# The last load group of a DMA-bound batched product: 112 rows and four pieces of 4 rows in place of 128 rows

## The chip, the cores and the metric

One core of one Trainium2 chip. The metric is the device time of one execution in microseconds (us); lower is better. The span of a profile is some 1.8 us shorter than the device time of the same run. Words used below: SBUF is the on-chip memory of 128 partitions, HBM the memory outside, SP the engine (SyncE) whose queue issues the DMAs; a row is what one DMA engine moves in one packet, to or from one partition; a landing is the event by which one DMA engine reports its share of a DMA as done, in us from the start of the span.

## The reference

```python
x: (8, 12, 512, 64) float32      y: (8, 12, 512, 64) float32
out = np.einsum('bhtc,bhsc->bhts', x, y)      # (8, 12, 512, 512) float32
```

25.2 MB are read and 100.7 MB written: 96 products of 512x64 by 64x512, each of which writes four times what it reads.

## The kernel before

The 96 heads are cut into 12 groups of 8. A group's x is 128 rows of 8 KB, one row per partition, and y likewise; both go into one slot of 16 KB per partition, of which there are five. Slots hold loads first and results afterwards. All DMAs are issued by SP.

```python
P = 128; G = 8; R = 32; NG = 12; SLOTS = 5        # C = 64, S = 512, K = 8
slots = ctx.enter_context(tc.tile_pool(name="slots", bufs=SLOTS))
...
def load(g):
    both = slot()
    nc.sync.dma_start(both[:, :R * C], xv[g])      # 128 rows of 8 KB
    nc.sync.dma_start(both[:, R * C:], yv[g])      # 128 rows of 8 KB
    loaded[g] = both
...
    # result(o): 8 matmuls, three copies from PSUM into a slot, and then
    return lambda: nc.sync.dma_start(ov[i, h], otf)    # 128 rows of 16 KB
...
for g in range(SLOTS):
    load(g)
...
for g in range(NG):                # compress each group to bf16 and load on
    ...
    if g < 5: load(g + SLOTS)
    elif g in (5, 7, 9): stores.append(result(len(stores)))
    elif g in (6, 8): load(g // 2 + 7)      # g == 8: the last group, 11
for store in stores:               # three finished results wait for the loads
    store()
for o in range(len(stores), 4 * NG):
    result(o)()
```

So all loads come first and all 48 stores after them, and group 11 is the last load on the queue.

## Time and profile before

| | before |
|---|---|
| time, 6 runs | 302.11 us (301.77 to 302.23) |
| profiled span | 300.3 us |
| bytes | 125.83 MB on one queue |
| a load row of 8 KB | 309 to 321 ns in one DMA engine |
| a store row of 16 KB | 611 ns in one DMA engine |

The prediction shows the lines that say that the DMA engines are the bound. One view is added here: the stretch in which the last loads run, cut into microseconds. Columns: stretch and length, busy time and count of PE, PEld, DVE, ACT and POOL, TensorE clock, mean busy share of the 16 DMA engines, GB/s. Kernel before:

```profile
57.00:58.00 1.00, 0.00 (x0) 0.00 (x0) 1.00 (x2) 0.92 (x2) 0.95 (x1) 0.50 0.99 410
58.00:59.00 1.00, 0.00 (x0) 0.00 (x0) 1.00 (x2) 1.00 (x2) 0.98 (x1) 0.50 1.08 451
59.00:60.00 1.00, 0.85 (x3) 0.30 (x3) 0.99 (x2) 1.00 (x2) 0.94 (x2) 0.50 0.97 401
60.00:61.00 1.00, 1.00 (x4) 0.34 (x3) 1.00 (x1) 1.00 (x2) 1.00 (x1) 0.50 1.06 442
61.00:62.00 1.00, 1.00 (x4) 0.33 (x3) 0.71 (x1) 0.98 (x2) 0.96 (x2) 0.50 1.00 401
62.00:63.00 1.00, 0.49 (x2) 0.10 (x1) 0.00 (x0) 1.00 (x1) 0.90 (x1) 0.97 1.22 508
63.00:64.00 1.00, 0.00 (x0) 0.00 (x0) 0.82 (x2) 0.98 (x2) 0.80 (x1) 1.00 0.92 393
64.00:65.00 1.00, 0.00 (x0) 0.00 (x0) 1.00 (x1) 0.97 (x2) 1.00 (x1) 1.00 0.92 393
```

A busy share above 1 only means that packets are counted in the slice in which they start.

### The profile page before, as it was taken

What the parts mean: (1) busy time and instruction counts of PE and PEld (TensorE: products, weight loads), DVE (VectorE), ACT (ScalarE), POOL (GpSimd) and SP (SyncE); (2) the same over time, 40 slices, a digit from 0 to 9 for tenths busy, and PEclk for the clock granted to TensorE, in tenths of its full rate; (3) what the DMA queues carried; (4) which work ended last, traced back from release to release, by engine and by line L of the source; (5) the groups of instructions that cost most, each with busy time, mean ns of one, the idle gap of its engine ahead of it and who ended that gap; (6) DMA issues with size and microseconds to landing.
All of it is one profiled execution on the core that took longest, in us unless ns stands there. A gap on an engine that the chain in (4) does not pass through costs nothing.

```text
span 300.3 us, 1412 instructions
## 1 busy us (share of the span) xinstructions
PE 145.4 (48%) x377; PEld 46.5 (15%) x384; DVE 182.6 (61%) x160; ACT 221.3 (74%) x169; POOL 59.1 (20%) x56
## 2 busy tenths in 40 slices
PE   0004044138657484856475656655674655673000
PEld 0001011012212121212121212211121211120000
DVE  1568895989984963947909649289195570603200
ACT  4666599998999779789789697888887977364000
POOL 2899999990000000000000000000000000000000
PEclk9999995676978659567957566779657788577555
DMA  7999999999999999999999999999999999999994
GB/s 281 430 421 421 422 423 420 426 429 440 421 431 436 419 436 434 421 436 432 420 450 423 423 439 423 432 439 421 436 432 423 426 438 423 420 421 441 426 430 205
DMA packets 10377, 125.93 MB, mean 419 GB/s; under 512 B 1152, under 2 KB 1152, under 8 KB 1152
## 3 DMA queue, kind: packets, MB, share of 16 engines
q1 hardware_dynamic: 10368, 125.83, 98.8%
q8 instruction: 3, 0.05, 0.1%
q14 instruction: 6, 0.05, 0.0%
HBM read 25.17 MB, written 100.66 MB: 419 GB/s over the span
## 4 chain that ended last, share of the span: by engine, by line
DMA 53%; ACT 11%; DVE 7%; issue 1%; DVEq 1%; PE 0%; ACTq 0%
DMA out_dram<-slot 53%; ACT slot L66 8%; DVE slot L68 7%; ACT xb L66 2%; ACT xk L83 1%; DVEq L192 1%; PE pm L135 0%; ACT yb L66 0%; DVE yb L68 0%; DVEq L68 0%; ACTq L66 0%
## 5 line engine op out<-in xcount | busy, mean ns | idle before, releaser
L135 PE MATMUL pm<-yT,xT 128*128 128x512 bf16 x377 | 145.4, 524 | 129.7 <-ACT slot L66 74.3
L66 ACT ACTIVATE slot<-pm 128x1536 f32<-128x1536 f32 (+1 forms) x108 | 133.2, 1314 | 37.9 <-DMA out_dram<-slot 27.7
L68 DVE COPY slot<-pm 128x1536 f32<-128x1536 f32 (+1 forms) x36 | 54.6, 1571 | 72.5 <-DMA out_dram<-slot 38.0
L135 PEld LDWEIGHTS <-xT 128*128 128x128 bf16 x384 | 46.5, 121 | 227.7 <-issue 194.0
L116 DVE STREAM_TRANSPOSE xT<-xb 128x1024 uint32<-128x1024 uint32 x24 | 48.8, 2034 | 6.2 <-PE pm L135 4.6
L66 ACT ACTIVATE xb<-xk 32x1024 bf16<-32x1024 bf16 x36 | 48.2, 1338 | 0.8
L68 DVE CAST yb<-slot 64x1024 bf16<-64x1024 f32 x24 | 33.8, 1408 | 17.6 <-DMA slot<-in_y_dram 17.3
L68 POOL COPY xb<-xk 32x1024 bf16<-32x1024 bf16 x24 | 38.5, 1606 | 1.2
L83 ACT ACTIVATE xk<-slot 128x2048 bf16<-128x2048 f32 x12 | 22.9, 1910 | 9.6 <-DMA slot<-in_x_dram 9.5
L68 DVE COPY xb<-xk 32x1024 bf16<-32x1024 bf16 x36 | 26.1, 725 | 0.4
L121 DVE STREAM_TRANSPOSE yT<-yb 128x512 uint32<-128x512 uint32 x24 | 25.1, 1044 | 0.0
L68 POOL CAST yb<-slot 64x1024 bf16<-64x1024 f32 x12 | 19.2, 1601 | 7.4 <-DMA slot<-in_y_dram 6.8
L66 ACT ACTIVATE yb<-slot 64x1024 bf16<-64x1024 f32 x12 | 15.9, 1329 | 3.6 <-DMA slot<-in_y_dram 3.5
L83 ACT ACT_TABLE_LOAD x1 | 1.3, 1283 | 0.7 <-PEq L181 0.7
L149 DVE MEMSET xb<- 128x64 uint32 x16 | 1.2, 112 | 0.8 <-PEq L181 0.8
L150 POOL MEMSET xb<- 128x64 uint32 x16 | 1.4, 151 | 0.3 <-POOLq L181 0.3
L181 POOL MEMSET const-float32-0.0<- 128x1 f32 x1 | 0.1, 98 | 0.2 <-issue 0.2
L181 POOL MEMSET const-float32-1.0<- 128x1 f32 x1 | 0.1, 98 | 0.0
L181 POOL MEMSET const-bfloat16-1.0<- 128x1 bf16 x1 | 0.1, 98 | 0.0
L181 POOL MEMSET const-uint8-127<- 128x1 uint8 x1 | 0.1, 98 | 0.0
## 6 DMA issues: line engine op xcount, KB each, us to landing
out_dram<-slot SPq DMA_DIRECT2D x48, 2048.0 KB, 20.6
slot<-in_x_dram SPq DMA_DIRECT2D x12, 1024.0 KB, 17.5
slot<-in_y_dram SPq DMA_DIRECT2D x12, 1024.0 KB, 19.3
```

Source lines behind the costliest of these rows:

```text
L66: nc.scalar.activation(dst, src, COPY)
L68: engine.tensor_copy(dst, src)
L83: nc.scalar.activation(xk.rearrange("p r c -> p (r c)"), both[:, :R * C], COPY)
L116: nc.vector.transpose(xT.rearrange("p (k r e) -> p k e r", k=K, e=E), xb.rearrange("p (k e c) -> p k e c", k=K, e=E),)
L121: nc.vector.transpose(yT.rearrange("p (r j) -> p j r", r=D), yb.rearrange("p (j c) -> p j c", c=D))
L135: nc.tensor.matmul(pm[:, j, :], xT[:, k + j, h, :], yT[:, h * S:(h + 1) * S], start=True, stop=True)
L149: nc.vector.memset(zeroed[0][:, k:k + 64], 0.0)
L150: nc.gpsimd.memset(zeroed[1][:, k:k + 64], 0.0)
L181: nc = _bacc.Bacc("TRN2", target_bir_lowering=False, num_devices=1)
L192: with _tile.TileContext(nc) as tc:
```

## The change

The intent follows from the sizes: the 16 DMA engines do not finish together, so 16 of the 128 rows of the last x and of the last y are taken off the even split and sent in pieces of 4 rows, each carried by four engines (that they are engines 0 to 3 is what the page says that the prediction cites, the records carry no numbers).

```diff
     def load(g):
         both = slot()
-        nc.sync.dma_start(both[:, :R * C], xv[g])
-        nc.sync.dma_start(both[:, R * C:], yv[g])
+        for src, dst in ((xv[g], both[:, :R * C]), (yv[g], both[:, R * C:])):
+            cuts = (0, P) if g < NG - 1 else (0, P - 16, P - 12, P - 8, P - 4, P)
+            for lo, hi in zip(cuts[:-1], cuts[1:]):
+                nc.sync.dma_start(dst[lo:hi], src[lo:hi])
         loaded[g] = both
```

## The prediction

> **What bounds the kernel now.** I read the page first: is one engine full, or the DMA?
>
> ```profile
> PE 145.4 (48%) x377; PEld 46.5 (15%) x384; DVE 182.6 (61%) x160; ACT 221.3 (74%) x169; POOL 59.1 (20%) x56
> ...
> DMA  7999999999999999999999999999999999999994
> ...
> q1 hardware_dynamic: 10368, 125.83, 98.8%
> ...
> DMA 53%; ACT 11%; DVE 7%; issue 1%; DVEq 1%; PE 0%; ACTq 0%
> ```
>
> No compute engine is over 74%, and the DMA row is full from the second slice to the next to last: the one queue's packets fill 98.8% of 16 engines' span. The chain names compute at places (ACT 11%), but only because compute waits for a slot which a store frees. So the span is start-up, 16 DMA engines' time for 125.83 MB, and a tail. The question for a change of 16 rows is how that work lies over the 16 engines, so I cut the end into pieces of 1 us (columns: stretch, then busy time and count of PE, PEld, DVE, ACT, POOL, clock, DMA share, GB/s):
>
> ```profile
> 290.00:296.00 6.00, 0.00 (x0) 0.00 (x0) 0.00 (x0) 0.00 (x0) 0.00 (x0) 0.50 1.02 434
> 296.00:297.00 1.00, 0.00 (x0) 0.00 (x0) 0.00 (x0) 0.00 (x0) 0.00 (x0) 0.50 0.23 98
> 297.00:298.00 1.00, 0.00 (x0) 0.00 (x0) 0.00 (x0) 0.00 (x0) 0.00 (x0) 0.50 0.15 66
> 298.00:299.00 1.00, 0.00 (x0) 0.00 (x0) 0.00 (x0) 0.00 (x0) 0.00 (x0) 0.50 0.04 16
> ```
>
> The engines do not end together: after 296 us some 4, then 2 to 3, then one of 16 still move data. The raw landing events say it more finely. Each DMA has 16 landings, one per engine. For the loads the first and last of them lie 0.32 to 0.36 us apart; for the last store ten engines land within 0.27 us, four at 0.90 to 1.06 us, one at 2.28 and one at 3.02 us. That one engine sets the end. The packet records say where its lag comes from: a store row (16 KB) takes 611 ns and a load row (8 KB) 309 ns, but three 16 KB instruction packets took 968, 967 and 948 ns, and single engines fall back by about as much when these pass. Engine numbers are not in the records.
>
> The last place to read is where the changed loads go, on the SP queue:
>
> ```profile
> 54.33 0.33 SPq L75 DMA_DIRECT2D slot<-in_x_dram  x1
> 54.71 0.42 SPq L76 DMA_DIRECT2D slot<-in_y_dram  x1
> 55.19 15.47 SPq L143 DMA_DIRECT2D out_dram<-slot  x4
> ```
>
> At 54.33 us the group before is still in the engines: landings complete at 55.37 (x of group 10), 57.84 (its y), 60.33 (x of group 11), 63.15 (its y), 68.02 us (store 0). No hole: 2.5 us per load (8 rows of 309 ns) and 4.87 per store (8 of 611).
>
> **What the Trainium skill says.** "DMA: Bandwidth & Descriptors", section "Why a DMA increments its semaphore by 16 and not by 1": a DMA is spread over the largest k up to 16 which divides its outer dimension, on the lowest-numbered k engines. 128 rows give 8 to each of 16, 112 give 7, and 4 rows go to engines 0 to 3, one each. The trace agrees for 128 rows (16 landings per DMA, 8 rows each); it has no 4-row DMA. The same page, "Latency and other measured facts", calls engines 7 and 15 usually slower, for a reason given as a guess. Two engines do lag most here, but nothing tells their numbers. "Runtime: NRT & Kernel Launch", section "Instruction fetch mechanics", has instruction memory refilled in 16 KiB blocks by the sequencer's own DMA queue; the three 16 KB packets are such blocks. "SBUF — State Buffer", section "Door 1: The DMA port swizzle", puts four neighbouring partitions on one DMA port, measured at 27.6 GB/s for partitions 0 to 3; no DMA of this trace is that narrow.
>
> **The change part by part.** The same bytes, otherwise dealt. Removed: two DMAs of 128 rows. Added: two of 112 and eight of 4, so 80 DMAs and not 72.
>
> 1. Rows. Per load, engines 4 to 15 get 7 and not 8; engines 0 to 3 get 7 + 4 = 11. For x and y together that is 2 rows less on twelve engines, 2 x 309 = 0.62 us, and 6 more on four engines, 6 x 309 = 1.85 us. The queue is never dry afterwards (a store takes 20.6 us from issue to landing, over four stores of 4.87), so these shifts should last to the end as lags do. If engines 0 to 3 are among the ten punctual ones, they end at up to 0.27 + 1.85 = 2.1 us on the old scale, the last laggard at 3.02 - 0.62 = 2.4: the end comes 0.6 us sooner. That is plainly the intent, and the size fits the measured lags well.
>
> 2. Issue. Eight more instructions on the SP queue, some 0.4 us each (0.33 to 0.42 above): 3.2 us, before the first store. The built order adds waits: eight semaphores are used in turn, so each DMA waits for the eighth before it. The third y piece waits for the 112 rows of x, the fourth for x's first piece, store 0 for x's second. From 57.84 us, x's 112 rows take 7 x 309 = 2.16 us, landing at about 60.0; the pieces follow 0.31 us apart, so the third y piece goes out at 60.1, the fourth at 60.5, store 0 at about 61.0. The first DMA of the run had its first packet 1.0 us after its issue began, so store 0 moves data from 62.0. Engines 4 to 15 have ended y's 112 rows at 60.0 + 2.16 = 62.2 on the landing clock, some 0.4 us earlier as packets (the last packet ends 0.46 us before the last landing). So they may stand dry 0.2 to 0.5 us, which eats half or more of the 0.6.
>
> 3. Later arrival. y of group 11 lands on engines 0 to 3 about 1.85 us later, near 65.0 us; VectorE waits for it (its cast starts at 63.17). Then store 3 moves from 70.1 to 72. Store 2 lands only at 77.8 us, so about 5 us of slack stay. Nothing comes of this.
>
> 4. Port. A piece of 4 rows is 32 KB into one port: at the skill's 27.6 GB/s an estimated 1.19 us, not 0.31. If four engines went in step through all eight pieces, that would be 8 x 0.88 = 7.0 us more on engines 0 to 3. But an engine ahead by some ns takes the next port alone, so the four should fan out: after about one piece they each have a port. I estimate 0.9 us (3 x 309 ns, a perfect fan) to 2.3 us.
>
> Sum: clean 302.11 - 0.62 + 0.3 = 301.8; with a fan of 0.9 us, engines 0 to 3 end at 0.2 + 1.85 + 0.9 = 2.95 against 3.02: 302.0. I take 302.1.
>
> **The rivals.** (a) A laggard is one of engines 0 to 3. Then the extra 1.85 us goes on top: 304.0 for the last one, 303.2 for the second (2.28 + 1.85 = 4.13 against 3.02). Two of 16 by blind draw: chance 45% that at least one falls in four, but whoever chose these sizes likely knew the lags, and the skill's 7 and 15 speak against; I give it 15%. (b) Ports in step: 0.2 + 1.85 + 7.0 = 9.05 against 3.02, so 308.1. For it: the skill's single-port figure. Against: the fan argument. In part, a fan of 2.3 us, 303.4. (c) SP waits leave engines 4 to 15 dry by over 1 us, which happens if x's second piece lands late by port sharing: the laggard keeps its 3.02 and gains perhaps 0.5: 302.6. (d) Nothing of it shows, since the laggards are moved by where instruction packets fall: 302.1.
>
> **Range and chances.** Clean or nearly so, 301.4 to 301.9: 35%. Even, to 302.4: 25%. Part port, part laggard, to 304.6: 30%. Above: 10%, of which the in-step case passes the 2% line at 308.15 only just. So 301.4 to 304.6, faster by over 2% (296.1) next to impossible: nothing here gives 6 us back.
>
> **What would show it.** Right: landings of the last store with the latest near 2.4 us after the first and four engines bunched near 2 to 3; the 4-row packets at 309 ns or, shared, up to 1.2 us; store 0 issued near 61 us and a shallow hole in the DMA share at 61 to 63 us, none later. Wrong: four engines ending 4 us or more after the rest (rivals a, b; the packets' length tells which), a hole of over 1 us before store 0 (c), or holes at store 3 (part 3).

## The result, and the profile after

| | before | after |
|---|---|---|
| time, 6 runs each | 302.11 us (301.77 to 302.23) | 305.32 us (304.52 to 305.66) |
| profiled span | 300.3 us | 303.9 us |
| bytes | 125.83 MB | 125.83 MB |

The ratio is 1.0104 (95% interval 1.009 to 1.0118): about 3.2 us slower, above the predicted range, though within the 2% that counts as the same. Ratios here are the mean time of one kernel's fast runs over that of the other's fast runs of the same rounds, so not quite the ratio of the medians quoted.

From the page of the changed kernel: the DMA row, the GB/s row, the queue, and the issues of the changed DMAs (name, count, KB of one, us to landing where given):

```profile
DMA  7999999999999999999999999999999999999995
GB/s 289 426 424 422 424 421 423 360 294 437 426 427 429 418 436 423 429 430 425 434 427 421 438 418 427 434 423 434 429 423 434 426 425 429 424 429 431 421 440 250
...
q1 hardware_dynamic: 10400, 125.83, 99.0%
...
slot<-in_x_dram SPq DMA_DIRECT2D x1, 896.0 KB
slot<-in_y_dram SPq DMA_DIRECT2D x1, 896.0 KB, 11.2
slot<-in_x_dram SPq DMA_DIRECT2D x4, 32.0 KB
slot<-in_y_dram SPq DMA_DIRECT2D x4, 32.0 KB
```

The busy row shows nothing: it is as full as before. The GB/s row shows it all: two slices, the eighth and ninth, move 360 and 294 GB/s where all their neighbours move over 420. The 32 packets more are the completion packets of the eight pieces. The same stretch in microseconds, changed kernel (columns as above):

```profile
57.00:58.00 1.00, 0.00 (x0) 0.00 (x0) 1.00 (x2) 0.92 (x2) 0.90 (x1) 0.50 1.02 303
58.00:59.00 1.00, 0.00 (x0) 0.00 (x0) 0.99 (x3) 1.00 (x2) 0.73 (x1) 0.50 1.02 287
59.00:60.00 1.00, 0.90 (x3) 0.34 (x3) 1.00 (x1) 1.00 (x2) 1.00 (x1) 0.50 1.06 311
60.00:61.00 1.00, 1.00 (x4) 0.31 (x3) 0.68 (x1) 1.00 (x2) 0.94 (x2) 0.50 1.12 262
61.00:62.00 1.00, 1.00 (x4) 0.29 (x2) 0.00 (x0) 0.98 (x2) 0.96 (x2) 0.50 1.18 197
62.00:63.00 1.00, 0.74 (x2) 0.15 (x1) 0.00 (x0) 1.00 (x1) 1.00 (x1) 0.50 0.81 164
63.00:64.00 1.00, 0.00 (x0) 0.00 (x0) 0.00 (x0) 0.97 (x2) 0.22 (x1) 0.50 1.03 205
64.00:65.00 1.00, 0.00 (x0) 0.00 (x0) 0.00 (x0) 0.69 (x2) 0.00 (x0) 0.50 0.92 295
```

Before, these eight microseconds moved 3399 (GB/s x us), after 2024. The difference, 1375, is 3.2 us at 425 GB/s, as much as the whole loss (what came after this stretch nearly cancels, see the landings below). And it is not idleness, since the busy share stays near 1 (0.81 to 1.18, 1.02 in the mean): the packets take longer. The packet records give the lengths. Median of the load rows that start in each microsecond, with smallest and largest, in ns (a load row is 8 KB in both kernels):

| us | before | after | what runs after |
|---|---|---|---|
| 56 | 314 (309 to 321) | 314 (309 to 321) | y of group 10, 128 rows |
| 57 | 309 (309 to 321) | 451 (316 to 522) | x's 112 rows begin |
| 58 | 314 (309 to 321) | 462 (435 to 562) | x's 112 rows |
| 59 | 311 (309 to 321) | 443 (432 to 522) | x's 112 rows |
| 60 | 314 (309 to 324) | 553 (424 to 760) | x's pieces, y's 112 rows |
| 61 | 312 (309 to 553) | 802 (647 to 1028) | the same |
| 62 | 312 (309 to 659) | 620 (580 to 760) | the same |
| 63 | stores only | 661 (512 to 988) | the same |
| 64 | stores only | 534 (488 to 661) | the last of them, first stores |
| 65 | stores only | 309 (309 to 502) | y's pieces, beside stores |

The step comes as the 112-row DMA begins, and the packets of all 16 engines take it. A second step comes with x's pieces. y's pieces, which run beside stores, are back at 309 ns.

The same in landing events (first of 16, us from the span's start): x of group 11 lands at 60.55 instead of 59.97, y's 112 rows at 64.95 where y had landed at 62.50, store 0 at 69.95 instead of 67.32. x's four pieces complete at 62.45, 63.30, 63.90 and 64.75, so 0.6 to 0.85 us apart; y's at 67.77, 68.10, 68.41 and 68.73, 0.31 to 0.33 apart.

The end, changed kernel, to be held against the three single microseconds that the prediction shows of before:

```profile
299.00:300.00 1.00, 0.00 (x0) 0.00 (x0) 0.00 (x0) 0.00 (x0) 0.00 (x0) 0.50 1.15 492
300.00:301.00 1.00, 0.00 (x0) 0.00 (x0) 0.00 (x0) 0.00 (x0) 0.00 (x0) 0.50 0.54 229
301.00:302.00 1.00, 0.00 (x0) 0.00 (x0) 0.00 (x0) 0.00 (x0) 0.00 (x0) 0.50 0.16 66
302.00:303.00 1.00, 0.00 (x0) 0.00 (x0) 0.00 (x0) 0.00 (x0) 0.00 (x0) 0.50 0.04 16
```

The tail is shorter than before, only later: the last store's landings lie 2.29 us apart instead of 3.02. The time was not lost to a longer tail.

For the experiments I read store 0 (all loads are over) and the last store in each trace: first, mean and last of the 16 landings, in us. The mean is what counts for lost capacity, the last for the end.

| kernel | store 0 first | mean | last | last store first | mean | last |
|---|---|---|---|---|---|---|
| before | 67.32 | 67.58 | 68.02 | 296.47 | 297.11 | 299.50 |
| after | 69.95 | 70.93 | 74.21 | 300.74 | 301.43 | 303.03 |

So the loss has three terms: 3.35 us until store 0 (means), 0.97 more from there to the last store (230.50 us against 229.53), and 0.79 regained because the tail from mean to last landing is shorter (1.60 against 2.39). Together 3.53, the shift of the last landing. In each of the 13 traces taken after the prediction the last landing moved as much as the mean of store 0 to within 0.52 us: a slower pace of the stores mostly goes with a shorter tail. The experiments therefore look for the first term.

### The profile page after: what moved, and what is told of

Same layout as the page of the kernel before. It is cut to its first block, busy times and chain, and to the rows that moved or that the text cites. A ratio compares the mean times of both kernels' runs of the same rounds, so it can differ in the third digit from the quotient of the medians.

```text
span 303.9 us, 1432 instructions
## 1 busy us (share of the span) xinstructions
PE 146.2 (48%) x384; PEld 46.5 (15%) x384; DVE 181.3 (60%) x160; ACT 221.5 (73%) x169; POOL 59.1 (19%) x56
## 3 DMA queue, kind: packets, MB, share of 16 engines
q1 hardware_dynamic: 10400, 125.83, 99.0%
## 4 chain that ended last, share of the span: by engine, by line
DMA 62%; ACT 17%; DVE 8%; issue 4%; PE 1%; DVEq 1%; SPq 0%; ACTq 0%
DMA out_dram<-slot 49%; ACT slot L67 12%; DMA slot<-in_y_dram 11%; DVE slot L69 5%; DMA slot<-in_x_dram 3%; ACT xk L86 2%; ACT xb L67 2%; DVE yb L69 2%; ACT yb L67 1%; PE pm L138 1%; DVE xT L119 1%; DVE yT L124 1%; DVEq L195 1%; SPq L79 0%; DVEq L69 0%
## 5 line engine op out<-in xcount | busy, mean ns | idle before, releaser
L69 DVE CAST yb<-slot 64x1024 bf16<-64x1024 f32 x24 | 31.9, 1328 | 23.5 <-DMA slot<-in_y_dram 23.3
```

Source lines behind the costliest of these rows:

```text
L69: engine.tensor_copy(dst, src)
```

## The experiments

Theory after the result: rows get longer because the narrow DMAs write SBUF partitions in a pattern in which several engines want the same port (a way into SBUF). The ports, in the expectations too, are those of the section that the prediction cites, "SBUF — State Buffer", "Door 1: The DMA port swizzle": four neighbouring partitions share a port, and 64 neighbouring ones reach 8 of 16. Rivals: the waits of SP that the many DMAs bring; the uneven load on engines 0 to 3 itself; the row counts as such, or HBM. Each kernel was timed in five rounds, beside the kernel before on the same chip (experiments 4, 7 and 10 have four times on record). The diffs are shortened to the lines that matter: those with - are the changed kernel's, and where there are none, only what the kernel of the experiment has instead is shown. Remarks after # are not in the code. Landings and rows are from one trace of each kernel.

**1. No pieces: 112 and 16 rows, both on all 16 engines.**

```diff
-            cuts = (0, P) if g < NG - 1 else (0, P - 16, P - 12, P - 8, P - 4, P)
+            cuts = (0, P) if g < NG - 1 else (0, P - 16, P)
```

> Theory (port sharing inside the 112-row DMA): with 112 rows the 16 DMA engines no longer each have a port of SBUF to themselves, so its 8 KB rows again take 440 to 470 ns and not 309, x of group 11 begins to land near 60.5 us and not 59.97; the 16-row rest lies on four ports and takes about 1 us. The time is 304 to 306 us although no engine gets more rows than another, and the landings of store 0 lie within about 1 us. Rival (only the 4-row pieces on engines 0 to 3 cost): the 112 rows take 309 ns, landing near 60.0 us, and the time is 302.0 to 302.5 us.

Measured: 305.57 us against 302.26, ratio 1.0123. No engine has more rows than another, SP has only two DMAs more, and the loss is as large as the change's. Kernel with 112 and 16 rows (columns as above):

```profile
57.00:58.00 1.00, 0.00 (x0) 0.00 (x0) 1.00 (x2) 0.92 (x2) 0.97 (x1) 0.50 1.10 328
58.00:59.00 1.00, 0.00 (x0) 0.00 (x0) 0.92 (x2) 1.00 (x1) 0.50 (x1) 0.50 1.05 262
59.00:60.00 1.00, 0.83 (x3) 0.28 (x3) 0.99 (x2) 1.00 (x2) 1.00 (x1) 0.50 0.95 262
```

The rows of the 112 had medians of 458, 523 and 476 ns in these microseconds, and x first landed at 60.92 (60.5 expected). Store 0 first, mean and last: 70.85, 71.61, 72.17, so a spread of 1.3 us where I expected about 1. The 112-row DMA stretches rows with no 4-row piece near it. The 16-row rest adds its own part: the rows of microsecond 61 took 694 to 1013 ns.

**2. The pieces over four port groups.** Every piece takes every fourth row.

```diff
-                nc.sync.dma_start(dst[lo:hi], src[lo:hi])          # the four pieces
+                for j in range(4):
+                    nc.sync.dma_start(dst[P - 16 + j:P:4], src[P - 16 + j:P:4])
```

> The four-row pieces take every fourth of the rows 112 to 127, so that the four rows of a piece lie in four port groups. Theory (ports): the pieces of x now take about 310 to 450 ns and land about 0.35 us apart and not 0.6 to 0.85; the 112 rows stay at 440 to 470 ns; about 1 us of the 3.2 comes back, 303.5 to 304.5 us. Rivals (the waits on the SP queue, or the six rows more on engines 0 to 3, cost the time): unchanged, 305.0 to 305.6 us.

Measured: 304.50 us against 302.26, ratio 1.0078, so 0.8 us of the 3.2 came back. x's pieces completed at 61.60, 62.27, 62.89 and 63.39: 0.5 to 0.7 us apart, better than neighbouring rows but not the 0.35 expected. The mean of store 0 fell from 70.93 to 70.12. Which rows a piece takes matters, but it is the smaller part. These pieces read separate rows of HBM too, as do those of 9 and 12, so here the written partitions are not the only thing that differs.

**3. The same shift of work, cut by columns.** 128 rows of 7 KB stay on 16 engines; the last eighth of the columns goes as one DMA of 124 rows and one of 4, whose greatest divisor up to 16 is 4 (the trace has four landings for each).

```diff
+                W = R * C * 7 // 8
+                nc.sync.dma_start(dst[:, :W], src[:, :W])
+                nc.sync.dma_start(dst[:P - 4, W:], src[:P - 4, W:])
+                nc.sync.dma_start(dst[P - 4:, W:], src[P - 4:, W:])
```

> All 128 rows go with 7/8 of their columns in one DMA on 16 engines, and the last eighth as one DMA of 124 rows and one of 4, which have only 4 as divisor and go to engines 0 to 3: the same shift of 128 KB per load, with the 128-row pattern kept. Theory (ports): rows of 7 KB at about 270 ns, no stretched stretch but for the short 1 KB rows, 301.5 to 302.3 us. Rival (the shift of work to engines 0 to 3 is itself what costs): 303.5 us or more.

Measured: 303.24 us against 302.26, ratio 1.0036: between the two expectations, so neither holds as stated. The 7 KB rows of x took 272 to 274 ns, no stretching, and x landed at 59.56. Store 0: first 67.44, mean 68.48, last 71.49: twelve engines lie within 0.43 us, and four come 3.14 to 4.05 us behind. At the end the first landing is 296.19, 0.28 us earlier than before, and the last 4.27 us after it. So here the uneven load does set the end: the first of the twelve gained 0.28, not the 0.62 of my sum, and the four overshot the old laggard. Small rows are part of that: 1 KB took 46 ns, where an eighth of an 8 KB row of 309 ns would be 39. y's 7 KB rows were stretched too, to a median of 459 ns in microsecond 61, while x's 1 KB rows ran beside them.

**4. Halves.** Two DMAs of 64 rows each.

```diff
+            cuts = (0, P) if g < NG - 1 else (0, P // 2, P)
```

> The last group's x and y go as two DMAs of 64 rows each, all on 16 engines with 4 rows each; no imbalance, no 4-row pieces. Theory (ports): 64 neighbouring partitions reach only half of the ports, so rows take up to about 600 ns, and the time grows to 304 to 307 us. Rival (what costs is a shape of 7 rows per engine, or the pieces): rows of 309 ns, 302.1 to 302.5 us.

Measured: 306.41 us against 302.26, ratio 1.0140. Kernel with halves (columns as above):

```profile
60.00:61.00 1.00, 1.00 (x4) 0.26 (x2) 0.85 (x1) 1.00 (x2) 0.94 (x2) 0.50 1.11 238
61.00:62.00 1.00, 1.00 (x3) 0.30 (x2) 0.00 (x0) 0.97 (x2) 1.00 (x1) 0.50 0.88 188
62.00:63.00 1.00, 0.66 (x2) 0.15 (x1) 0.00 (x0) 1.00 (x1) 0.96 (x2) 0.50 1.08 246
```

Half the bytes at full busy share, and row medians of 549 to 629 ns: close to twice 309. Each half takes 2.3 to 2.7 us (first landings), about as long as a whole 128-row DMA (2.5).

**5. Halves by every second partition.** The same two reads of 64 neighbouring rows from HBM, written to partitions 0, 2, 4 and so on, then 1, 3, 5. Its output is wrong, which doesn't matter for the time.

```diff
+                for j in range(2):
+                    nc.sync.dma_start(dst[j:P:2], src[j * (P // 2):(j + 1) * (P // 2)])
```

> Wrong result on purpose (rows of the last group land in other partitions). As in the kernel with halves, the last x and y go as two DMAs of 64 rows, read from the same 64 neighbouring rows in HBM, but written to every second partition, so that each DMA reaches all ports. Theory (what stretches rows is which partitions are written): rows between 309 and about 500 ns once the engines have moved apart, 303 to 305.5 us. Rival (the row count of a DMA or the HBM side stretches them): rows of 611 to 620 ns and 306.2 to 306.6 us as with the halves.

Measured: 302.27 us against 302.16, ratio 1.0006 (0.9994 to 1.0019); nothing is left of the loss, better than the theory's own numbers. Kernel with every second partition:

```profile
60.00:61.00 1.00, 1.00 (x4) 0.27 (x3) 1.00 (x1) 1.00 (x2) 1.00 (x1) 0.50 0.99 410
61.00:62.00 1.00, 1.00 (x3) 0.30 (x2) 0.59 (x1) 0.98 (x2) 0.96 (x2) 0.50 1.11 459
62.00:63.00 1.00, 0.70 (x2) 0.15 (x1) 0.00 (x0) 1.00 (x1) 0.78 (x1) 0.50 1.06 442
```

In the microseconds 57 to 60 all load rows take 309 to 322 ns. Between 4 and 5 the DMAs, their number, the rows per engine and the bytes read are the same; only the partitions written differ. That rules out HBM, the row count and the number of DMAs for the halves.

**6. The column cut for y alone.**

```diff
+            if g < NG - 1 or src is not ys:     # x of the last group in 128 rows too
+                nc.sync.dma_start(dst, src)
```

> The column cut for y alone, half the shift of work to engines 0 to 3. Theory: in the kernel with the cut of both, the four engines fell 3.1 to 4.0 us behind, past the old laggard's 3.0; with half of it they fall some 1.6 to 2 us behind and no longer set the end, while the other twelve gain about 0.15 us: 301.8 to 302.4 us. Rival (the small DMAs themselves cost in proportion): half of the 1.0 us of the whole cut, 302.7 to 302.9 us.

Measured: 302.01 us against 302.16, ratio 0.9996 (0.9982 to 1.0009): as the theory said, but no gain either. x is not cut here, and y's rows of 7 KB took 272 to 275 ns (medians), not stretched. Half of the work is moved, so the prediction's sum is 0.31 us and not 0.62; the first landing came 0.30 us sooner at store 0, which agrees. Store 0: first 67.02, last 69.21, with four engines 1.3 to 2.2 us behind. At the end the first landing is at 296.12, 0.35 earlier than before, but one engine is 3.21 us behind it, so the last is at 299.33 against 299.50. This is the best version I have of the change's idea, and it does not beat the kernel before beyond the noise.

**7. The change for x alone.**

```diff
-            cuts = (0, P) if g < NG - 1 else (0, P - 16, P - 12, P - 8, P - 4, P)
+            cuts = (0, P) if g < NG - 1 or n else (0, P - 16, P - 12, P - 8, P - 4, P)   # n: 0 for x, 1 for y
```

> The change for x alone; y goes in 128 rows. Theory (each 112-row DMA and its pieces stretch rows on their own): the mean landing of store 0 moves by about half of 3.35 us, 1.3 to 2.0 us, and the time is 303.2 to 304.2 us. Rival (the SP waits of the third and fourth y piece and of store 0, which are gone here): nearly all of the loss is gone, 302.1 to 302.6 us.

Measured: 305.14 us against 302.16, ratio 1.0104. Both expectations missed: nearly the whole loss is there with half of the change. The mean of store 0 is 70.74 (after: 70.93). Kernel with x alone:

```profile
61.00:62.00 1.00, 1.00 (x4) 0.29 (x2) 0.00 (x0) 0.97 (x2) 0.96 (x2) 1.00 0.82 123
62.00:63.00 1.00, 0.76 (x2) 0.15 (x1) 0.00 (x0) 1.00 (x1) 1.00 (x1) 1.00 0.97 156
63.00:64.00 1.00, 0.00 (x0) 0.00 (x0) 0.00 (x0) 0.98 (x2) 0.19 (x1) 1.00 0.94 172
```

These are y's plain 128 rows, beside x's pieces: rows of 835, 804 and 732 ns (medians), on all engines. So the second step in the changed kernel comes from x's pieces hitting whatever load follows them, be it 112 or 128 rows, and y's own pieces cost little beside the stores (cutting y too moves the mean of store 0 by 0.19 us only). SP's waits for the y pieces are gone here and the loss stays, which rules them out.

**8. Extra pieces only.** All loads in 128 rows; between the last x and y six extra pieces of 4 neighbouring rows, 5 KB each, go to a spare buffer.

```diff
+            nc.sync.dma_start(dst, src)
+            if g == NG - 1 and n == 0:
+                for lo in range(P - 24, P, 4):
+                    nc.sync.dma_start(spare[lo:lo + 4], src[lo:lo + 4, :1280])
```

> All 128-row DMAs stay as before; between the last x and y six extra DMAs of 4 neighbouring rows (5 KB each, together 30 KB on each of engines 0 to 3) go to a spare buffer, so pieces stand beside y's 128 rows with no 112-row DMA near. Theory (x's pieces, each written into one port, slow the rows of all engines that are loading beside them): y's rows take 500 to 900 ns, the landings of twelve engines for store 0 come 1.5 to 2.5 us later, 303.5 to 305 us. Rival (the 112-row shape starts the trouble, and pieces alone hold up only engines 0 to 3): twelve engines land store 0 as before, within 0.3 us, four lie 1.2 to 3 us behind, 302.0 to 302.8 us.

Measured: 303.94 us against 301.89, ratio 1.0066, and the first landing of store 0 at 69.13, 1.81 us later. Kernel with extra pieces:

```profile
60.00:61.00 1.00, 1.00 (x4) 0.32 (x3) 1.00 (x1) 1.00 (x2) 1.00 (x1) 0.50 1.21 183
61.00:62.00 1.00, 1.00 (x4) 0.29 (x2) 0.72 (x1) 0.97 (x2) 0.96 (x2) 0.50 1.09 172
62.00:63.00 1.00, 0.74 (x2) 0.15 (x1) 0.00 (x0) 1.00 (x1) 0.90 (x1) 0.50 0.83 156
```

y's rows had medians of 843, 819 and 678 ns in these microseconds, and none of those that began in 60 to 62 took less than 746. The theory holds: pieces alone, with no 112-row DMA near, slow all engines. The extra bytes explain little: six rows of 196 ns on 4 of 16 engines are 0.29 us in the mean, and the mean moved by 2.25.

**9. The same extra pieces, rows 6 apart.**

```diff
+                for lo in range(P - 24, P - 18):
+                    nc.sync.dma_start(spare[lo:P:6], src[lo:P:6, :1280])
```

> As the kernel with extra pieces, but each piece takes four rows 6 apart, in four port groups. Theory (one port for a whole piece is what hurts): most of the loss is gone, twelve engines land store 0 within 0.8 us of before, 302.0 to 303.0 us. Rival (any 4-row DMA beside a load hurts, whichever partitions it writes): the same time as with neighbouring rows, within 0.4 us.

Measured: 303.32 us against 301.89, ratio 1.0044. Above what the theory allowed and 0.62 under the kernel of 8, more than the rival allowed; the first landing of store 0 at 68.30 is 0.98 later than before. The pieces took about 200 ns (medians 202 and 196), but ten 8 KB rows that began beside them in the half microsecond from 59.5 took 720 to 1228 ns. But this run has a fault of its own: a piece with separate rows holds SP for 0.66 us (3.95 us for the six) and not 0.34, so y was issued at 58.65 us, and the DMA share between 60.0 and 60.5 fell to 0.44. Inconclusive, so experiments 11 and 12 repeat it with three pieces.

**10. Pieces last.** x's 112 rows, y's 112 rows, then the eight pieces.

```diff
+            nc.sync.dma_start(dst[:P - 16], src[:P - 16])       # x, then y; then, for both,
+                for lo in range(P - 16, P, 4):
+                    nc.sync.dma_start(dst[lo:lo + 4], src[lo:lo + 4])
```

> The same DMAs as in the changed kernel, in another order: x's 112 rows, y's 112 rows, then the eight pieces, which now run beside stores and not beside loads. Theory (the 112 rows cost about 1 us each, the pieces of x some 2 us because y's load runs beside them, and pieces beside stores nearly nothing): the mean landing of store 0 moves by 1.7 to 2.6 us and not 3.35, and the time is 303.5 to 304.6 us. Rival (the cost of pieces does not depend on what runs beside them): 305.0 to 305.6 us.

Measured: 306.69 us against 301.89, ratio 1.0161, slower than any expectation. The order makes a new wait: the last pieces and store 0 wait on SP for semaphores of DMAs not yet done, and store 0 is issued only at 65.68 us. Kernel with pieces last:

```profile
64.00:65.00 1.00, 0.00 (x0) 0.00 (x0) 0.00 (x0) 0.64 (x1) 0.00 (x0) 1.00 0.27 74
65.00:66.00 1.00, 0.00 (x0) 0.00 (x0) 0.73 (x1) 0.00 (x0) 0.74 (x1) 1.00 0.22 90
66.00:67.00 1.00, 0.00 (x0) 0.00 (x0) 0.00 (x0) 0.24 (x1) 1.00 (x1) 0.56 0.40 164
```

This is what an idle queue looks like: the busy share falls with the GB/s, to 0.22. In the changed kernel it did not. The run still gives one clean number: with no piece beside them, x's and y's 112 rows took from 57.33 to 64.32 us (first landings), 6.99 us, where 2 x 7 rows of 309 ns take 4.33. The 112-row DMAs cost 1.3 us each on their own.

**11 and 12. Three extra pieces, neighbouring rows and rows 6 apart.** As 8 and 9, with `range(P - 12, P, 4)` and `range(P - 24, P - 21)`. y is now issued at 55.76 and 56.82 us, while x still runs.

> Three extra pieces of 4 neighbouring rows (5 KB each) between the last x and y, so that y can be issued before the engines run out, which in the run with six strided pieces it was not. Theory (pieces written into one port slow the load beside them): about half of the 1.8 us that six pieces cost the first landing of store 0, 0.7 to 1.2 us, and y's rows again at 500 ns or more for a while; 302.6 to 303.3 us. Rival (pieces cost only by the late issue of y): store 0 first lands within 0.3 us of before.

> The same three pieces with their rows 6 apart. Theory (a piece over four ports costs its bytes alone): rows of y near 309 to 350 ns, first landing of store 0 within 0.3 us of before and the time 301.7 to 302.4 us. Rival (any 4-row DMA beside a load hurts): as with neighbouring rows, within 0.3 us.

Measured: 303.13 us with neighbouring rows and 302.60 us with separate ones, against 301.80 (ratios 1.0039 and 1.0026). The first landing of store 0 moved by 0.65 and 0.35 us, both just outside what was expected; the means by 0.91 and 0.55, of which 0.15 is bytes (three rows of 196 ns on 4 of 16 engines). y's rows went up to a median of 808 ns in the half microsecond from 60.0 with neighbouring rows and to 552 ns with separate ones. So by these means about half of what the pieces cost beyond their bytes hangs on their rows being neighbours (0.76 against 0.40 us). That is an estimate from one trace each: the ranges of the times touch (302.79 to 303.33 and 302.51 to 302.87), and of the rival's "within 0.3 us" the first landing just keeps to it (0.30) while the time does not (0.53). Why separate rows still cost something I have not taken apart further.

## Why the prediction was wrong

The prediction gave 302.1 us in 301.4 to 304.6; measured were 305.32.

**The bound.** Right: the DMA engines' time is what counts, and nothing on the compute side came of it. Store 3 was issued at 74.25 us, later than the 72 given, and no hole followed.

**Part 1, rows.** The sum holds where rows are not stretched, which in the changed kernel they are. Experiment 6 moves half of the work, 0.31 us by the same sum, and the first landing came 0.30 us sooner at store 0 and 0.35 at the last store. Experiment 3 moves all of it, but stretched y's rows, and 0.28 of the 0.62 was left at the end. The statement that a shift lasts to the end as lags do fails in the changed kernel: its four late engines were 2.74 to 4.25 us behind the first at store 0, but the whole spread at the last store was 2.29 us. The leading engines took 230.78 us from store 0 to the last store, against 229.15 before, with store rows of 615.5 ns in the mean instead of 613.1 (from 80 us on). I have not found what sets that rate. One reading of the prediction was off, though nothing hung on it: the 0.32 to 0.36 us between first and last landing hold for all loads but the last, y of group 11, which has 0.64.

**Part 2, issue.** The step that made the prediction wrong starts here: "x's 112 rows take 7 x 309 = 2.16 us". They took 3.17 us (57.38 to 60.55). I carried the duration of a row of a 128-row DMA over to a DMA of another shape, which the trace of before did not contain. Store 0 was issued at 63.31 us and not 61.0, for the same reason. The feared dry spell of engines 4 to 15 did not come, since these engines were themselves late: y's 112 rows landed at 64.95 at the earliest.

**Part 4, port.** The mechanism that the halves bear out, in the wrong place. I let ports slow engines 0 to 3 alone, and only in the pieces. In fact two terms were missing, and both fall on all engines:

| term | predicted | measured |
|---|---|---|
| x's 112 rows | 2.16 us | 3.17 us |
| y's 112 rows, with x's pieces beside them | 2.16 us | 4.40 us (60.55 to 64.95) |
| their sum, against two 128-row DMAs of before (57.48 to 62.50, 5.02 us) | -0.70 us | +2.55 us |

The shift of store 0's first landing, +2.63 us, is this sum less 0.10 us at its start (57.38 against 57.48) and 0.19 more in store 0 itself (5.01 against 4.82). The fan argument itself shows in y's pieces: 0.31 to 0.33 us apart at 309 ns each, beside stores. x's pieces, beside loads, did not fan out freely, at 0.6 to 0.85 us apart.

**Rivals.** (a) fits in form but did not set the time: four engines do fall behind, but the spread at the end is shorter than before. (Against it I had put what the skill says of engines 7 and 15; the same entry calls its guessed reason specific to the SWDGE path, DMAs issued from GpSimd, and all DMAs here are issued from SP, so it counted for less.) (b), all ports in step, did not happen. (c) and (d) did not happen. The signs I named were partly met by luck, for another reason: "the latest near 2.4 us after the first" was met with 2.29, but not with four engines bunched near 2 to 3, and the hole at 61 to 63 us was there in GB/s (197 and 164) but not in busy share (1.18 and 0.81). I had looked for idle engines and got slow ones.

**What is shown and what is not.** Shown: 112-row DMAs stretch rows by themselves (1.3 us each in experiment 10, 1.0 in the changed kernel; also 1); pieces beside a load stretch that load's rows on all engines (7, 8, 11); for halves it is the written partitions and nothing else (4 against 5), and for pieces, rows being neighbours looks like about half of it (11 against 12, an estimate; partitions and HBM rows change together there). Read together with the port table in "Door 1" of "SBUF — State Buffer", the likely cause is engines meeting at SBUF ports. For the 112 rows this is argued and not shown: no run writes 112 rows to other partitions, and a part of HBM or of the row count (7 per engine) is ruled out for the halves alone. "DMA: Bandwidth & Descriptors", section "Back-pressure in remote DMA", offers a reason why a few engines may slow others: a saturated SBUF port clogs the path back to the engines that write through it and to those that share that path. It is written for transfers between cores; the rows of 800 ns on all engines beside pieces of four look like it, but no run here shows the path. Open stay which engine takes which of 112 rows, why separate rows still cost something, and the slower pace of the stores afterwards (0.97 us in the mean).

## What to carry to other kernels

A row's duration belongs to the shape of its DMA: do not carry the 309 ns of a 128-row load over to 112, 64 or 4 neighbouring rows, and do not count a narrow DMA as costing its own engines alone: here it slowed the full-width loads beside it. When a queue is full, look at GB/s beside the busy share; the loss here was invisible in the one and plain in the other. Evening out the engines' finish by moving rows is worth at most the time from the mean of the last landings to the last (2.39 us here), and the one way found to do it without stretched rows, by columns of y, gained nothing measurable.

## What the Trainium skill lacked or had wrong

- "SBUF — State Buffer", section "Door 1: The DMA port swizzle", judges a range by how many of the 16 ports it covers. By its table 112 rows cover all 16, yet their rows took 443 to 523 ns (medians) instead of 309. For 64 neighbouring partitions it is right: half the ports, row medians of 549 to 629 ns. It has no measurement of stepped partitions. By its formula 64 rows at every second partition reach all 16 ports, and here they ran at full rate, 309 to 322 ns, at 1.0006 of the time.
- "DMA: Bandwidth & Descriptors", section "Rules for kernel authors", says that two transfers to disjoint partition halves serialize because both use the same 16 engines. Its advice to use one 128-partition transfer holds, but the reason falls short: halves were worse than serial here, +4.15 us for two loads, and sharing the engines is not why, since the same halves over every second partition share them too and cost nothing (1.0006).
- The same page's section "Why a DMA increments its semaphore by 16 and not by 1" agrees with the traces: a 4-row DMA shows one early event and four landings. What a DMA on few engines does to full loads beside it is on no page that I found: y's 8 KB rows rose to medians of 678 to 843 ns beside six pieces.
- No page that I found says how long SP takes to issue a DMA of a given shape: 4 rows held it 0.34 us apiece with neighbouring rows and 0.66 with rows 6 apart, 128 rows 0.33 to 0.44 at this place. It is not the step alone, for 64 rows took 0.57 to 0.60 us, neighbouring or at every second partition.
